# A decoder layer on one core: the residual row before the FFN is formed with the norm's weight multiplied ahead, its transposed float32 copy is taken first, and rows 512 to 1023 go first

## The chip, the core and the metric

The kernel runs on one core of a Trainium2 chip. A core has five engines that work side by side, each through its own instructions in a fixed order: PE (matrix products and transposes), DVE, ACT and POOL (elementwise work) and SP, which issues the DMA transfers here. The products go to PSUM, the other operands lie in SBUF. The metric is the time of one execution in microseconds (us), and lower is better.

## The reference, cut to what matters

```python
def rms_norm(x, g):
    y = xf * lax.rsqrt(jnp.mean(xf * xf, axis=-1, keepdims=True) + NORM_EPS)
    return (y * g.astype(jnp.float32)).astype(x.dtype)
...
mix = hybrid_mixer(rms_norm(h, g_mix_pre[i]), ...)          # ends in concat([attn, c]) @ w_o
h = h + rms_norm(mix, g_mix_post[i])
ffn = conv_gated_ffn(rms_norm(h, g_ffn_pre[i]), ...)
h = h + rms_norm(ffn, g_ffn_post[i])
...
def conv_gated_ffn(xn, w_gate, w_up, dw_w, dw_b, w_down):
    g = causal_depthwise_conv(xn @ w_gate, dw_w, dw_b)       # 3 taps along the sequence
    return (jax.nn.gelu(g, approximate=True) * (xn @ w_up)) @ w_down
```

There are 1024 positions of width 1024, in float32, and D_FF is 2816. The part at stake here is the end of the mixer (the product with `w_o` and the post norm), the residual, the pre norm of the FFN, and the first products of the FFN.

## The kernel before, in words

Each float32 operand of a product is split into a rounded high part and a low part, so that one product becomes three. The 1024 positions are eight rows of tiles of 128 positions; here they are called row 0 to row 7 in the order in which they are worked on, and in the kernel before that is also their place in the sequence. Rows 0 to 3 form one half of 512 positions (`xh[1]`, `xl[1]` serve as `hh[0]`, `hl[0]`), rows 4 to 7 the other (`hh1`, `hl1`).

The program is written for a scheduler, which fixes each engine's order at build time. So the order of the listing is not the order on an engine; the orders quoted below are those of the built programs.

For each row, `wo_mm` makes 24 products on PE into one of two PSUM buffers `ps_w`. Their rounded inputs `ch` (ACT) and `cl` (POOL, four subtractions of 128x128) have two buffers. `wo_post` and `back_h` then do this, and the letters are used from here on:

- **A** (L915, DVE): the partial row from DRAM is added to `ps_w`, which frees the PSUM buffer.
- **J** (L179 on `junk`, ACT): the mean square. **P** (L169, L170, POOL): its reciprocal root, two small instructions.
- **X**: the row of the residual. Before, this is L917 on DVE (`part` times root times weight), and then L918 on POOL (`xr` plus `part`).
- **S** (L179 on `part`, ACT) and **Q** (L169, L170, POOL): the same for the second norm. **F** (L922, DVE): the row times root times weight, into `tmp`.
- **T** (L929, PE): eight transposes into one of two PSUM buffers `ps_h`.
- **H** (L118, ACT): the rounded part `hh`. **L** (L123, DVE): the low part `hl`. **C** (L931, ACT): the float32 copy of the transposed row into `acc`, which is stored to `hT_d`.

The last two rows' T are held back (`late`) behind the first products of the FFN. Those are four sets of 48 products: gate and up of FFN tile 0 (`g0`, `u0`), gate and up of tile 11 (`g1`, `u1`), each set over both halves of the positions, 24 products each. After them the FFN goes over to seven products in place of eight (the first is `ps_ga`). These need sums of blocks of the transposed rows, which `block_sums(j)` on DVE makes from `hT_d[j]` and `hT_d[4 + j]`, read back from DRAM; `sal` is the last kind of block that they write. On DVE the same queue holds the three-tap convolution of the gate (`conv3`, L1092 behind ACT's L1090).

Of the kernel before, what the change touches and what calls it, by code (L numbers as in the profile page):

```python
# [15 lines left out]
F32 = mybir.dt.float32  # L16
# [3 lines left out]
ALU = mybir.AluOpType  # L20
# [72 lines left out]
def layer_kernel(tc, x, xT, pT, pos, vecs, rows, w_inc, w_q, w_kv, w_qb, w_kvb, w_o, w_gu, w_down, w_ple, w_pg, out):  # L93
    nc = tc.nc
    pools = {}

    def popen(name, side="left", space=None):
        kw = dict(name=name, bufs=1, reuse_waits="tile")
        if space is not None:
            kw["space"] = space  # L100
        kw["side"] = side
        cm = tc.tile_pool(**kw)
        pools[name] = (cm, cm.__enter__())
        return pools[name][1]
# [11 lines left out]
    def split(src, hi, lo, scale=None, leng=None):  # L116
        if scale is None:
            nc.scalar.copy(hi, src)  # L118
        else:
            nc.scalar.activation(out=hi, in_=src, func=AF.Copy, scale=scale)  # L120
        if scale is None:
            e = nc.gpsimd if leng == "pool" else nc.vector
            e.tensor_tensor(out=lo, in0=src, in1=hi.bitcast(F32), op=ALU.subtract)  # L123
        else:
            nc.vector.scalar_tensor_tensor(out=lo, in0=src, scalar=scale, in1=hi.bitcast(F32), op0=ALU.mult, op1=ALU.subtract)  # L125

    def mm(ps, l, r, st, sp):
        nc.tensor.matmul(ps, lhsT=l, rhs=r, start=st, stop=sp)  # L128
# [37 lines left out]
    def rstd_of(ms, tag, mul=None):  # L166

        t = small.tile([P, 1], F32, name="rs", tag="rs" + tag, bufs=3)
        nc.gpsimd.tensor_scalar(out=t, in0=ms, scalar1=1.0, scalar2=EPS, op0=ALU.mult, op1=ALU.add)  # L169
        nc.gpsimd.tensor_tensor(out=t, in0=t, in1=mhalf[:, 0:1], op=ALU.pow)  # L170
        if mul is not None:
            nc.gpsimd.tensor_scalar(out=t, in0=t, scalar1=mul, scalar2=0.0, op0=ALU.mult, op1=ALU.add)
        return t

    def msq(src, junk, n, tag, out=None):

        if out is None:
# [17 lines left out]
    acc = [accp.tile([P, S], F32, name=f"acc{m}") for m in range(NCH)]  # L195
# [95 lines left out]
    with tc.high_priority():  # L291
        ps = psv("ps_x")
        for t in range(NT):
            tk = slice(t * P, (t + 1) * P)
# [57 lines left out]
    for i in range(2, 2 * NCH):  # L352
        w = nw
# [30 lines left out]
    def trt(n, **kw):  # L384
        return trg.tile([P, NT, NFQ], F32, name=n, **kw)
# [21 lines left out]
    for a, i, levels in ((al, 3, 0), (ah, 3, 0), (al, 2, 0), (ah, 2, 1), (al, 1, 1), (ah, 1, 1), (al, 0, 1), (ah, 0, 2)):  # L407
        q = trt("pr", tag="pr", bufs=2)
# [20 lines left out]
    def ps1(name):  # L429
        return psA.tile([P, HALF], F32, name=name, tag="s1", bufs=2)  # L430
# [91 lines left out]
    for nm, wh, wl, width, rank, dh, dl in (("k", wkh, wkl, KVW, KVL, kah, kal), ("q", wqh, wql, QL, QL, qah, qal)):  # L522
        stages = []
        for t in range(NT):
            g, tk = t // 4, slice(t % 4 * P, (t % 4 + 1) * P)
# [85 lines left out]
    with tc.high_priority():  # L611
        V2(out=y1, in0=x1, in1=cosT, op=ALU.mult)
        for g in range(2):
            sl = slice(g * HALF, (g + 1) * HALF)
            tmp = ps1("ps_t")
# [275 lines left out]
    def psd(name, i):  # L891
        return psB.tile([P, D], F32, name=name, tag=f"d{i % 2}", bufs=2)
# [3 lines left out]
    hh = [xh[1], hnp.tile([P, KD, HALF], F32R, name="hh1")]  # L896
    hl = [xl[1], hnp.tile([P, KD, HALF], F32R, name="hl1")]
    hp = popen("hp")
    gmix = hp.tile([P, D], F32, name="gmix")
    nc.sync.dma_start(gmix, rows[0:1, :].partition_broadcast(P))  # L900
    gffn = hp.tile([P, D], F32, name="gffn")
    nc.sync.dma_start(gffn, rows[1:2, :].partition_broadcast(P))

    def wo_mm(t):
        ps = psd("ps_w", 0)
        part = hp.tile([P, D], F32, name="part2", tag="part2", bufs=3)
        nc.sync.dma_start(part, mix_d[t])
        xr = hp.tile([P, D], F32, name="xr", tag="xr", bufs=3)
        nc.sync.dma_start(xr, x[t * P:(t + 1) * P, :])
        halves = [slice(0, HALF), slice(HALF, D)]  # L910
        wo_products(ps, list(zip(halves, halves)), 0, *rows_of(0, t, hp, 2))
        return ps, part, xr

    def wo_post(t, ps, part, xr):
        nc.vector.tensor_tensor(out=part, in0=ps, in1=part, op=ALU.add)  # L915
        r = rstd_of(msq(part, pools["wop"][1].tile([P, D], F32, name="junk", tag="rawo", bufs=2), D, "w"), "w")
        nc.vector.scalar_tensor_tensor(out=part, in0=part, scalar=r, in1=gmix, op0=ALU.mult, op1=ALU.mult)  # L917
        nc.gpsimd.tensor_tensor(out=xr, in0=xr, in1=part, op=ALU.add)  # L918
        nc.sync.dma_start(h_d[t], xr)
        r = rstd_of(msq(xr, part, D, "w"), "w")  # L920
        tmp = hp.tile([P, D], F32, name="tmp", tag="tmp", bufs=2)
        nc.vector.scalar_tensor_tensor(out=tmp, in0=xr, scalar=r, in1=gffn, op0=ALU.mult, op1=ALU.mult)  # L922
        return tmp

    def back_h(t, tmp):
        g, tk = t // 4, slice(t % 4 * P, (t % 4 + 1) * P)
        pst = psd("ps_h", 1)
        for k in range(KD):
            nc.tensor.transpose(out=pst[:, k * P:(k + 1) * P], in_=tmp[:, k * P:(k + 1) * P], identity=ident)  # L929
        split(pst.rearrange("p (j q) -> p j q", q=P), hh[g][:, :, tk], hl[g][:, :, tk])  # L930
        nc.scalar.copy(acc[2 + t % 2], pst)  # L931
        nc.sync.dma_start(hT_d[t], acc[2 + t % 2])

    hT_d = dram.tile([NT, P, D], F32, name="hT_d")
    late = []
    nxt = wo_mm(0)
    for t in range(NT):
        cur = nxt
        if t + 1 < NT:
            nxt = wo_mm(t + 1)  # L940
        turned = wo_post(t, *cur)
        if t < NT - 2:
            back_h(t, turned)
        else:
            late.append((t, turned))
# [256 lines left out]
    junk = dp.tile([P, D], mybir.dt.bfloat16, name="junk")  # L1202
# [115 lines left out]
    def h2_trans(t):  # L1318
        pst = psE.tile([P, D], F32, name="ps_ht", tag="ht", bufs=1)
        for k in range(KD):  # L1320
            nc.tensor.transpose(out=pst[:, k * P:(k + 1) * P], in_=h2[t][:, k * P:(k + 1) * P], identity=ident)  # L1321
        th_, tl_ = (t_.rearrange("p (k c) -> p k c", c=P) for t_ in h2b[t % 2])
        split(pst.rearrange("p (j q) -> p j q", q=P), th_, tl_)
        return th_, tl_

    with tc.high_priority():
        nxt = h2_trans(0)
    for t in range(NT):
        th_, tl_ = nxt
        if t + 1 < NT:  # L1330
            nxt = h2_trans(t + 1)
# [3 lines left out]
        r = rstd_of(msq(et, sg, D, "e"), "e", mul=0.5)  # L1335
# [68 lines left out]
```

## Time and profile before

| | |
|---|---|
| times of three runs | 1291.3, 1291.8 and 1297.38 us, median 1291.8 us |
| the profiled execution's own time | 1292.91 us, span from first to last instruction 1291.1 us |
| PE busy | 1230.6 us, 95% of the span |
| DVE, ACT, POOL busy | 71%, 48%, 43% |
| mean granted PE clock | 0.972 of full speed |

The profile is of one execution. An engine that is busy for 95% of the span sets the time nearly everywhere; where it stands still or gets a lower clock, something is to be won. A stage can be bounded by another engine than the whole is, so stages are read by themselves.

### The profile page before, as it was taken

What the parts mean: (1) busy time and instruction counts of PE and PEld (TensorE: products, weight loads), DVE (VectorE), ACT (ScalarE), POOL (GpSimd) and SP (SyncE); (2) the same over time, 40 slices, a digit from 0 to 9 for tenths busy, and PEclk for the clock granted to TensorE, in tenths of its full rate; (3) what the DMA queues carried; (4) which work ended last, traced back from release to release, by engine and by line L of the source; (5) the groups of instructions that cost most, each with busy time, mean ns of one, the idle gap of its engine ahead of it and who ended that gap; (6) DMA issues with size and microseconds to landing.
All of it is one profiled execution on the core that took longest, in us unless ns stands there. A gap on an engine that the chain in (4) does not pass through costs nothing. (4 is left out here: it accounts for less than half of the span.)

```text
span 1291.1 us, 16697 instructions
## 1 busy us (share of the span) xinstructions
PE 1230.6 (95%) x5905; PEld 1032.9 (80%) x5905; DVE 919.2 (71%) x1192; ACT 625.0 (48%) x1117; POOL 553.1 (43%) x588
## 2 busy tenths in 40 slices
PE   9999999889999989699999999999999999997998
PEld 7789987778888878577788888888888888885887
DVE  8399999865566545678887787787777876687343
ACT  6346775576656645454333433333334444463122
POOL 4776954542633348526546555565511200013000
PEclk9999999799999989889999999999999999998999
DMA  6210146534643256554322323331369544452232
GB/s 232 66 54 1 45 164 218 160 110 140 158 105 90 82 191 209 204 168 151 122 97 84 106 87 117 122 121 59 123 215 339 159 142 135 138 169 74 66 98 66
DMA packets 58483, 167.41 MB, mean 130 GB/s; under 512 B 6880, under 2 KB 10336, under 8 KB 56864
## 3 DMA queue, kind: packets, MB, share of 16 engines
q1 hardware_dynamic: 58256, 166.23, 39.4%
q8 instruction: 46, 0.75, 0.3%
q14 instruction: 37, 0.30, 0.1%
q10 hardware_dynamic: 144, 0.12, 0.0%
HBM read 114.42 MB, written 51.90 MB: 129 GB/s over the span
## 5 line engine op out<-in xcount | busy, mean ns | idle before, releaser
L343 DVE SCALAR_TENSOR_TENSOR ps_cv<-c,hvec,ps_cv 128x1023 f32<-128x1023 f32 (+25 forms) x96 | 122.2, 1273 | 2.6
L169 POOL TENSOR_SCALAR rs<-ss 128x1 f32<-128x1 f32 x32 | 16.2, 508 | 242.9 <-ACT junk L179 136.4
L717 POOL TENSOR_SCALAR pr<-pr,sm 128x896 f32<-128x896 f32 (+3 forms) x64 | 47.8, 751 | 123.1 <-DVE sm L716 100.6
L118 ACT CAST xh<-acc 128x512 fp32r<-128x512 f32 x77 | 47.9, 622 | 96.3 <-PE ps_da L1241 42.3
L123 POOL TENSOR_TENSOR kt<-acc,qt 128x512 fp32r<-128x512 f32 x39 | 62.9, 1620 | 43.0 <-ACT qt L118 31.3
L128 PE MATMUL ps_s<-kt,qt 96*128 96x512 f32 (+3 forms) x288 | 71.2, 377 | 9.2 <-ACT pr L715 6.1
L123 POOL TENSOR_TENSOR hl<-acc,hh 128x512 fp32r<-128x512 f32 x40 | 61.5, 1544 | 38.0 <-ACT hh L118 26.3
L1092 DVE SCALAR_TENSOR_TENSOR gt<-gx,vec,gt 128x1023 f32<-128x1023 f32 (+1 forms) x40 | 64.7, 1634 | 13.5 <-ACT gt L1090 13.5
L123 DVE TENSOR_TENSOR xl<-acc,xh 128x512 fp32r<-128x512 f32 x77 | 52.7, 687 | 29.8 <-ACT xh L118 28.6
L1241 PE MATMUL ps_da<-xl,xh 128*128 128x512 f32 x176 | 68.6, 390 | 0.4 <-DVE xl L123 0.4
L1241 PE MATMUL ps_da<-xh,xl 128*128 128x512 f32 x176 | 68.5, 389 | 0.0
L123 DVE TENSOR_TENSOR ptl<-ps_pt,pth 128x512 fp32r<-128x512 f32 (+2 forms) x96 | 50.9, 551 | 23.7 <-ACT pth L118 22.9
L1241 PE MATMUL ps_da<-xh 128*128 128x512 f32 x176 | 66.7, 389 | 0.0
L128 PEld LDWEIGHTS ps_s<-kt,qt 96*128 96x128 f32 x288 | 50.9, 201 | 18.1 <-ACT pr L715 8.4
L715 ACT ACTIVATE pr<-ps_s,mx,qf 128x896 f32<-128x896 f32 (+3 forms) x64 | 53.5, 839 | 22.8 <-DVE mx L712 21.5
L710 DVE TENSOR_REDUCE mx<-ps_s 128x1 f32<-128x896 f32 (+3 forms) x64 | 46.9, 752 | 24.0 <-PE ps_s L128 23.7
L118 ACT CAST pth<-ps_pt 128x512 fp32r<-128x512 f32 (+2 forms) x96 | 43.8, 485 | 25.0 <-PE ps_pt L727 24.6
L128 PE MATMUL ps_pg<-wg 128*128 128x512 f32 x192 | 47.6, 408 | 4.9 <-ACT wg L118 4.9
L128 PE MATMUL ps_c<-xl,wch 128*128 128x512 f32 x128 | 51.6, 404 | 0.3 <-DVE xl L125 0.3
L128 PE MATMUL ps_c<-xh,wcl 128*128 128x512 f32 x128 | 51.4, 401 | 0.0
L1241 PE MATMUL ps_db<-xh,xl 128*128 128x512 f32 x132 | 51.4, 389 | 0.0
L123 POOL TENSOR_TENSOR wx<-acc,wx 128x512 fp32r<-128x512 f32 x21 | 33.4, 1594 | 41.9 <-ACT wx L118 34.8
(623 smaller groups left out, 4007.2 us busy)
## 6 DMA issues: line engine op xcount, KB each, us to landing
acc<-in_w_gu_dram SPq DMA_DIRECT2D x44, 512.0 KB, 4.7
acc<-act_d SPq DMA_DIRECT2D x77, 256.0 KB, 2.8
act_d<-gx SPq DMA_DIRECT2D x22, 512.0 KB, 3.1
bw<-in_w_down_dram SPq DMA_DIRECT2D x32, 256.0 KB, 5.9
act_d<-gt SPq DMA_DIRECT2D x11, 512.0 KB, 2.6
kn_d<-wq SPq DMA_DIRECT2D x8, 512.0 KB, 3.2
qn_d<-wq SPq DMA_DIRECT2D x8, 512.0 KB, 3.7
kt<-kn_d SPq DMA_DIRECT2D x8, 512.0 KB, 5.3
```

The lines of the kernel that those rows point to most:

```text
L118: nc.scalar.copy(hi, src)
L123: e.tensor_tensor(out=lo, in0=src, in1=hi.bitcast(F32), op=ALU.subtract)
L128: nc.tensor.matmul(ps, lhsT=l, rhs=r, start=st, stop=sp)
L169: nc.gpsimd.tensor_scalar(out=t, in0=ms, scalar1=1.0, scalar2=EPS, op0=ALU.mult, op1=ALU.add)
L343: nc.vector.scalar_tensor_tensor(out=pc[:, s_:], in0=c[m][:, :S - s_], scalar=tap(m, s_), in1=pc[:, s_:], op0=ALU.mult, op1=ALU.add)
L710: nc.vector.tensor_reduce(out=mx, in_=ps, axis=AX.X, op=ALU.max, negate=True)
L715: nc.scalar.activation(out=pr[:, :n], in_=ps, func=AF.Exp, scale=qfi, bias=mx, accum_out=sm)
L717: nc.gpsimd.tensor_scalar(out=pr[:, :n], in0=pr[:, :n], scalar1=sm, scalar2=0.0, op0=ALU.mult, op1=ALU.add)
L1092: nc.vector.scalar_tensor_tensor(out=out[:, s_:], in0=src[:, :S - s_], scalar=V("dw", 3 * f + 2 - s_), in1=out[:, s_:], op0=ALU.mult, op1= ...
L1241: nc.tensor.matmul(bank[j], lhsT=l[:, js], rhs=r, start=first and kk == n == 0, stop=kk == HF - 1 and n == 2, skip_group_check=not first)
```

## The change

`wo_post` multiplies the row by the norm's weight in an instruction of its own (called **G** below, L922 after), which needs no root and so can run while ACT makes the mean square. The residual X is then one instruction on DVE (L923), `tmp` times root plus `xr`, and POOL's addition is gone. Of the transposed row the float32 copy C comes first; H and L read this copy in SBUF in place of the PSUM tile. The rows are worked on in the order 4, 5, 6, 7, 0, 1, 2, 3, and the halves of the first FFN products change places with them. Every fourth row has a `part` buffer of its own, and the scratch for J is one fixed buffer.

```diff
+    ROWS = (4, 5, 6, 7, 0, 1, 2, 3)
+    junk_w, part_x = (pools["wop"][1].tile([P, D], F32, name=n, tag="rawo", bufs=2) for n in ("junk", "partx"))
...
-        part = hp.tile([P, D], F32, name="part2", tag="part2", bufs=3)
+        part = part_x if t % 4 == 3 else hp.tile([P, D], F32, name="part2", tag="part2", bufs=3)
...
-        r = rstd_of(msq(part, pools["wop"][1].tile([P, D], F32, name="junk", tag="rawo", bufs=2), D, "w"), "w")
-        nc.vector.scalar_tensor_tensor(out=part, in0=part, scalar=r, in1=gmix, op0=ALU.mult, op1=ALU.mult)
-        nc.gpsimd.tensor_tensor(out=xr, in0=xr, in1=part, op=ALU.add)
+        tmp = hp.tile([P, D], F32, name="tmp", tag="tmp", bufs=2)
+        r = rstd_of(msq(part, junk_w, D, "w"), "w")
+        nc.vector.tensor_tensor(out=tmp, in0=part, in1=gmix, op=ALU.mult)
+        nc.vector.scalar_tensor_tensor(out=xr, in0=tmp, scalar=r, in1=xr, op0=ALU.mult, op1=ALU.add)
...
-        split(pst.rearrange("p (j q) -> p j q", q=P), hh[g][:, :, tk], hl[g][:, :, tk])
-        nc.scalar.copy(acc[2 + t % 2], pst)
-        nc.sync.dma_start(hT_d[t], acc[2 + t % 2])
+        row = acc[2 + t % 2]
+        nc.scalar.copy(row, pst)
+        nc.sync.dma_start(hT_d[t], row)
+        split(row.rearrange("p (j q) -> p j q", q=P), hh[g][:, :, tk], hl[g][:, :, tk])
...
-    ffn_mm(*g0, 0)
-    ffn_mm(*u0, 0)
+    ffn_mm(*g0, 1)
+    ffn_mm(*u0, 1)
...
-    ffn_mm(*g1, 0)
+    ffn_mm(*g1, 1)
     u1 = psd("ps_u", 1), wu_
     for pw in (g0, u0, g1):
-        ffn_mm(*pw, 1)
-    for g in range(2):
+        ffn_mm(*pw, 0)
+    for g in (1, 0):
         ffn_mm(*u1, g)
```

DVE, late rows of the stage. Before, in the built order, the queue holds F (L922), X's first half (L917) and L (L123 from `ps_h`):

```order
L922 SCALAR_TENSOR_TENSOR tmp<-xr,rs,gffn 128x1024
L917 SCALAR_TENSOR_TENSOR part_5235<-part_5235,rs,gmix 128x1024
L123 TENSOR_TENSOR hl_4841<-ps_h,hh_4840 128x8x128
L922 SCALAR_TENSOR_TENSOR tmp<-xr,rs,gffn 128x1024
L917 SCALAR_TENSOR_TENSOR part_5304<-part_5304,rs,gmix 128x1024
```

The same queue after the change, for rows 4 and 5, holds X (L923), L, A (L919), F (L926) and G (L922) in this order:

```order
L923 SCALAR_TENSOR_TENSOR xr<-tmp,rs,xr 128x1024
L123 TENSOR_TENSOR hl_4841<-acc_103,hh_4840 128x8x128
L919 TENSOR_TENSOR part_5163<-ps_w,part_5163 128x1024
L926 SCALAR_TENSOR_TENSOR tmp<-xr,rs,gffn 128x1024
L922 TENSOR_TENSOR tmp<-part_5163,gmix 128x1024
L923 SCALAR_TENSOR_TENSOR xr<-tmp,rs,xr 128x1024
```

So a row has five instructions of full size on DVE in place of four, of which only A still reads PSUM, and L of an older row and A of the next one stand between a row's X and its F.

ACT, the same rows. Before, H (L118 from `ps_h`) comes first and C (L931) after S or J of the next rows:

```order
L118 CAST xh_125<-ps_h 128x8x128
L179 ACTIVATE part_5097,ss<-xr 128x1024
L179 ACTIVATE junk,ss<-part_5166 128x1024
L931 COPY acc_104<-ps_h 128x1024
L179 ACTIVATE part_5166,ss<-xr 128x1024
```

After, S and J are followed by C (L935) and, at once, by H, which reads the copy `acc`:

```order
L179 ACTIVATE part_5095,ss<-xr 128x1024
L179 ACTIVATE junk,ss<-part_5163 128x1024
L935 COPY acc_104<-ps_h 128x1024
L118 CAST hh_4840<-acc_104 128x8x128
L179 ACTIVATE part_5163,ss<-xr 128x1024
```

C no longer stands behind L of its own row, and with it `ps_h` is free.

PE, where the last products of `g1` (weights in `qt`, `kt`; rows in `xh_125`, `xl_127` or `hh_4840`, `hl_4841`) give way to `u1`. Before, all 48 products of `u1` stand here, first those with `xh_125`:

```order
L128 MATMUL ps_g<-hh_4840,kt 128x512
L128 MATMUL ps_u<-xh_125,qt 128x512
L128 MATMUL ps_u<-xl_127,qt 128x512
L128 MATMUL ps_u<-xh_125,kt 128x512
L128 MATMUL ps_u<-xh_125,qt 128x512
```

After the change the first 23 products of `u1` stand elsewhere, behind the first half of `g1` and the last T (L933):

```order
L128 MATMUL ps_g<-hh_4840,qt 128x512
L128 MATMUL ps_g<-hl_4841,qt 128x512
L128 MATMUL ps_g<-hh_4840,kt 128x512
L933 MATMUL ps_h<-ident,tmp 128x128 x8
L128 MATMUL ps_u<-hh_4840,qt 128x512
L128 MATMUL ps_u<-hl_4841,qt 128x512
```

Behind them come 97 products up to `ps_ga`, those of the second half; the last of `g1` is the 74th of them, and 23 products of `u1` follow it in place of 48.

## Rows read from the trace of the kernel before

**Rows 1.** Windows of the stage: busy us (instructions) per engine, granted clock, DMA.

```profile
466.00:516.00 50.00, 48.89 (x224) 40.47 (x224) 22.02 (x19) 23.63 (x58) 36.30 (x54) 0.96 0.53 182
516.00:554.00 38.00, 26.02 (x110) 20.47 (x109) 23.44 (x21) 17.93 (x25) 16.94 (x18) 0.83 0.58 212
```

**Rows 2.** Timeline of PE: start, duration, instruction, [idle before it, releaser].

```profile
520.83 0.76 PE L128 MATMUL ps_g<-xh,wfh 128*128 128x512 f32 x1 [4.67 <-DVE part L915]
...
549.20 1.97 PE L929 MATMUL ps_h<-ident,tmp 128*128 128x128 f32 x8 [4.79 <-ACT acc L931]
552.27 0.79 PE L128 MATMUL ps_g<-hh,wfh 128*128 128x512 f32 x1 [1.10 <-ACT hh L118]
...
558.36 0.40 PE L128 MATMUL ps_g<-hh,wfh 128*128 128x512 f32 x1
...
571.28 0.39 PE L128 MATMUL ps_g<-hh,kt 128*128 128x512 f32 x1
...
582.39 0.39 PE L1086 MATMUL ps_ga<-xh,wx 128*128 128x512 f32 x1
...
589.70 0.50 PE L1086 MATMUL ps_gb<-sal,qt 128*128 128x512 f32 x1 [1.03 <-DVE sal L123]
...
622.59 0.50 PE L1086 MATMUL ps_ud<-sah,qt 128*128 128x512 f32 x1 [2.19 <-DVE v L1018]
```

**Rows 3.** Timeline of POOL, ACT and DVE: one round of the late rows.

```profile
533.26 2.40 POOL L918 TENSOR_TENSOR xr<-xr,part 128x1024 f32<-128x1024 f32 x1 [1.40 <-DVE part L917]
...
535.70 1.06 ACT L179 ACTIVATE part<-xr 128x1024 f32<-128x1024 f32 x1 [0.33 <-POOL xr L918]
...
537.79 1.28 DVE L922 SCALAR_TENSOR_TENSOR tmp<-xr,rs,gffn 128x1024 f32<-128x1024 f32 x1 [3.47 <-POOL rs L170]
...
537.98 1.15 POOL L169 TENSOR_SCALAR rs<-ss 128x1 f32<-128x1 f32 x1 [0.22 <-ACT junk L179]
...
539.79 1.29 DVE L917 SCALAR_TENSOR_TENSOR part<-part,rs,gmix 128x1024 f32<-128x1024 f32 x1 [0.71 <-POOL rs L170]
...
541.15 2.40 POOL L918 TENSOR_TENSOR xr<-xr,part 128x1024 f32<-128x1024 f32 x1 [1.40 <-DVE part L917]
```

**Rows 4.** Timeline of DVE and POOL: rows 0 to 3.

```profile
474.61 1.23 DVE L915 TENSOR_TENSOR part<-ps_w,part 128x1024 f32<-128x1024 f32 x1 [7.74 <-PE ps_w L128]
474.72 1.73 POOL L123 TENSOR_TENSOR cl<-att,ch 128x128 fp32r<-128x128 f32 x4 [4.81 <-ACT ch L118]
...
477.11 0.19 POOL L169 TENSOR_SCALAR rs<-ss 128x1 f32<-128x1 f32 x1 [0.67 <-ACT junk L179]
...
477.96 1.28 DVE L917 SCALAR_TENSOR_TENSOR part<-part,rs,gmix 128x1024 f32<-128x1024 f32 x1 [2.12 <-POOL rs L170]
...
505.68 1.47 DVE L917 SCALAR_TENSOR_TENSOR part<-part,rs,gmix 128x1024 f32<-128x1024 f32 x1 [0.71 <-POOL rs L170]
```

**Rows 5.** Timeline of POOL and DVE where both have SBUF operands at once.

```profile
516.12 2.35 POOL L918 TENSOR_TENSOR xr<-xr,part 128x1024 f32<-128x1024 f32 x1 [1.40 <-DVE part L917]
...
517.10 2.46 DVE L123 TENSOR_TENSOR kt<-acc,qt 128x1024 fp32r<-128x1024 f32 x1
...
520.61 1.21 DVE L123 TENSOR_TENSOR kt<-acc,qt 128x1024 fp32r<-128x1024 f32 x1
...
590.78 4.23 POOL L123 TENSOR_TENSOR kt<-acc,qt 128x512 fp32r<-128x512 f32 x1 [6.43 <-ACT qt L118]
...
593.19 0.68 DVE L1018 TENSOR_TENSOR gx<-gt,gx 128x512 f32<-128x512 f32 x1
```

**Rows 6.** Timeline of ACT and DVE: last copies, block sums and convolution; row 7's A.

```profile
527.82 1.23 DVE L915 TENSOR_TENSOR part<-ps_w,part 128x1024 f32<-128x1024 f32 x1 [2.48 <-DMA part<-mix_d]
...
553.51 1.01 ACT L931 COPY acc<-ps_h 128x1024 f32<-128x1024 f32 x1 [1.29 <-DVE hl L123]
...
572.01 1.20 ACT L1090 ACTIVATE gt<-ps_g,vec 128x1024 f32<-128x1024 f32 x1
...
574.85 1.27 DVE L1092 SCALAR_TENSOR_TENSOR gt<-ps_g,vec,gt 128x1023 f32<-128x1023 f32 x1
```

More of the change, by code (lines that the diff above doesn't have):

```diff
@@ L915, in wo_post @@
         nc.vector.tensor_tensor(out=part, in0=ps, in1=part, op=ALU.add)
-        r = rstd_of(msq(part, pools["wop"][1].tile([P, D], F32, name="junk", tag="rawo", bufs=2), D, "w"), "w")
-        nc.vector.scalar_tensor_tensor(out=part, in0=part, scalar=r, in1=gmix, op0=ALU.mult, op1=ALU.mult)
-        nc.gpsimd.tensor_tensor(out=xr, in0=xr, in1=part, op=ALU.add)
+        tmp = hp.tile([P, D], F32, name="tmp", tag="tmp", bufs=2)
+        r = rstd_of(msq(part, junk_w, D, "w"), "w")
+        nc.vector.tensor_tensor(out=tmp, in0=part, in1=gmix, op=ALU.mult)
+        nc.vector.scalar_tensor_tensor(out=xr, in0=tmp, scalar=r, in1=xr, op0=ALU.mult, op1=ALU.add)
         nc.sync.dma_start(h_d[t], xr)
         r = rstd_of(msq(xr, part, D, "w"), "w")
-        tmp = hp.tile([P, D], F32, name="tmp", tag="tmp", bufs=2)
         nc.vector.scalar_tensor_tensor(out=tmp, in0=xr, scalar=r, in1=gffn, op0=ALU.mult, op1=ALU.mult)
@@ L929, in back_h @@
             nc.tensor.transpose(out=pst[:, k * P:(k + 1) * P], in_=tmp[:, k * P:(k + 1) * P], identity=ident)
-        split(pst.rearrange("p (j q) -> p j q", q=P), hh[g][:, :, tk], hl[g][:, :, tk])
-        nc.scalar.copy(acc[2 + t % 2], pst)
-        nc.sync.dma_start(hT_d[t], acc[2 + t % 2])
+        row = acc[2 + t % 2]
+        nc.scalar.copy(row, pst)
+        nc.sync.dma_start(hT_d[t], row)
+        split(row.rearrange("p (j q) -> p j q", q=P), hh[g][:, :, tk], hl[g][:, :, tk])
     hT_d = dram.tile([NT, P, D], F32, name="hT_d")
     late = []
-    nxt = wo_mm(0)
-    for t in range(NT):
+    nxt = wo_mm(ROWS[0])
+    for n, t in enumerate(ROWS):
         cur = nxt
-        if t + 1 < NT:
-            nxt = wo_mm(t + 1)
+        if n + 1 < NT:
+            nxt = wo_mm(ROWS[n + 1])
         turned = wo_post(t, *cur)
-        if t < NT - 2:
+        if n < NT - 2:
             back_h(t, turned)
```

## The prediction, made before the changed kernel was run

> **What bounds the kernel now.** The page's first view has PE busy for 95% of the span, so only a stage in which PE stands or runs slowly can give time back. The windows show such a stage just where the change is made: PE is busy for 48.89 of 50 us while the products with `w_o` run, but for 26.02 of 38 us from 516 to 554, at a mean granted clock of 0.83 [rows 1]. PE's timeline says what it stood for [rows 2]: 4.67 us for A of row 6, whose `ps_w` buffer `g0` needs; 4.79 us for C of row 6, without which the last T has no `ps_h` buffer; then 1.10 and 1.03 us. Behind the second of these PE was at the lower level (1.2 GHz): the 14 products from 552.27 to 558.36 took 6.09 us, while the 57 from 558.36 to 571.28 took 12.92 us, 0.227 each, at 2.4 GHz. That is 2.9 us lost beside the idle time.
>
> Both waits are on the chain of the rows' norms, which runs over DVE, ACT and POOL. A late round of it goes from POOL's addition at 533.26 to the next at 541.15, 7.89 us [rows 3]: addition 2.40, S 1.24, then J on ACT, whose root P gives X its start 0.72 us after F has ended (537.79 + 1.28 to 539.79). For rows 0 to 3, with `cl` on POOL as well, L917 recurs from 477.96 to 505.68 in three rounds of 9.24 us [rows 4]. PE needs only 24 x 0.227 = 5.4 us for a row's products and some 0.8 for a T (an estimate: half of the 1.97 at the lower level in rows 2, less its overlapped end), 6.2 together. So the chain is the slower one, and PE runs out of buffers.
>
> **The change, part by part.** *X without POOL, G aside.* POOL's 2.40 us leave the chain. X is one instruction on DVE, of L917's kind, 1.28. G costs 1.21, as the subtraction at 520.61 with the same shape and two SBUF inputs [rows 5]. It can run beside J, but the built order puts it behind F.
>
> *What the two engines do to each other.* An operation with two SBUF inputs on DVE and an operation on POOL do not run at once: `kt` on DVE takes 2.46 us while POOL's addition of 516.12 is under way, and 1.21 us alone; POOL's 590.78 subtraction takes 4.23 us, until DVE's unbroken row of additions ends at 593.87 [rows 5]; P's first instruction takes 1.15 us beside F [rows 3], and 0.19 alone [rows 4]. A, with PSUM, does not do this: `cl` took 1.73 us for four beside it [rows 4]. After the change G and L (now from the copy in SBUF) belong to the kind that excludes POOL, so a row has four such instructions, 1.28 + 1.21 + 1.28 + 1.21 = 5.0 us, where it had two.
>
> The Trainium skill, "SBUF — State Buffer", section "Who interferes with whom", states it as an exclusive lock on a port pair for the whole instruction, for VectorE operations with two SBUF inputs against GpSimd operations that read SBUF, and not for one with a PSUM input. The trace agrees with the numbers just given. By this rule alone the change would gain nothing while `cl` runs: the pair's work per row would stay at about 8.2 us (before 2 x 1.28 + 1.73 + 1.46 + 2.40, after 5.0 + 1.73 + 1.46). That result is the second rival below; without the rule it is the first.
>
> *The round after.* Take X's start as zero. DVE goes on with L and A, without a wait, until 3.55; S (1.24) ends at 2.55, Q (0.85, as from 477.11 to 477.96 [rows 4]) fits beside A and ends at 3.45; F ends at 4.8, G at 5.95. J follows A and ends at 4.85, but P must wait for G and gives X its start 0.72 later: a round of 6.65 us against 7.89. With `cl`, which comes ahead of Q on POOL and finds room only from A's start at 2.4, Q ends 1.5 us later and the round is 8.1 against 9.24. So X starts at 478.5 for row 0 (0.5 behind L917's 477.96, as G and `cl` exclude each other), at about 485.9 and 492.9 (no L yet), 501, 509.1 and 517.1 (with `cl`), 526.2 (two subtractions `kt` of 1.21 and their casts lie between) and 533.6. The last F ends at 538.4.
>
> *PE.* The products of row n + 2 need A of row n. A of rows 4, 5 and 6 ends at 504.7, 512.8 and 520.9, so PE stands three times for 1.6 to 1.9 us. Then: 24 products and a T to 527.2, `u0` to 532.6, the next T behind F to 533.8, `g1` to 539.2, the last T to 540.0. Its C (1.01 [rows 6]) frees the buffer of `u1` at 541.1; 23 products end at 546.4, and the 97 of the second half at 568.4. `ps_ga` began at 582.39 [rows 2]: 14.0 us are won up to there.
>
> *C first.* The 4.79 us wait goes, as T no longer waits for H, L and C in a row. What is late next is F, by 0.3 us, and then `u1` by 1.1.
>
> *The halves and `u1`.* Here the gain is cut. The block sums hang on the last C, at 541.1 against 554.52 [rows 6], 13.4 us earlier. But DVE's third convolution instruction (574.85) needs all of `g1`, and only 23 products of `u1` follow `g1` now, in place of 48. `g1` is complete at 546.4 + 74 x 0.227 = 563.2, ACT's 1.20 us [rows 6] follow, and the instruction starts at 564.5: only 10.35 us earlier. The activation behind it takes 0.45 more, and DVE has no gap from there to `sal`. So `ps_gb` gets `sal` at 579.8 against 589.70 [rows 2], 9.9 us earlier, while PE is there at 568.4 + 25 x 0.227 = 574.1. PE's new wait is 5.7 us. It will bring a stretch at the lower level, which costs 2 to 3 us if the one in rows 2 is a measure; but the next wait was 2.19 us at 622.59 [rows 2], for DVE's chain, and this takes it up. Two products of `ps_gd` that stood ahead of the wait stand behind it (0.45), and I leave 0.25 for the rest. Net 9.2.
>
> *At no cost:* the `part` buffer. A of row 7 waited 2.48 us for its load [rows 6]; now the load is issued behind S of row 3, some 15 us ahead of need. The same 512 KB transfers run as before, C's store is issued earlier, and what covers this is that A of row 7 is not what PE waits for; were it late, each us would move the last three T.
>
> *Sum:* 1292.91 - 9.2 = 1283.7 us. The profiled execution is 1.1 us (0.1%) above the median of 1291.8, too little to correct for.
>
> *Bounds.* The prices that no row shows are what DVE and POOL lose to each other and what POOL gets between two DVE instructions. Below: nothing lost, then rows go at PE's 6.2 us. Above: rounds as long as before, 9.24 and 7.89. I take 8.1 and 6.65, as the shares that exclude each other are measured, and the row of 590.78 shows POOL held over several DVE instructions. Ends: 1277.9 and 1289.2, worked out next.
>
> **Rivals.** *PE sets the pace.* If the exclusion costs nothing that PE notices, `g0` starts at 515.6, the second half at 540.6 and `g1` is complete 5.8 us earlier than above: 1283.7 - 5.8 = 1277.9. If the convolution isn't late either, the whole 19.8 us at `ps_ga` stay: 1273.1. For it speaks that POOL loses 2.40 us a row; against it that DVE alone has five instructions, some 6 us, a row.
>
> *The pair of engines sets the pace, no change to be measured.* Rounds stay at 9.24 and 7.89. Then X of row 7 comes at 539.1, 5.5 us later than in the sum, and the time is 1289.2; with the late convolution weighing more, up to 1298. For it speaks the equal sum of 8.2 us; against it that the round of before was longer than that sum, so that the chain, which is cut, counted too.
>
> *The clock, slower than before.* PE stands three times between 503 and 521. If the level falls there and stays low, each us of it costs half a us of products. The gain of 9.2 is gone after 18.4 us at 1.2 GHz, and after 31.4 us the kernel is slower by 0.5%, 1298.4. For it: the windows had 0.83 over 38 us [rows 1]. Against it: the 1.03 us wait at 589.70 is followed by matmuls at full rate, and the level fell behind waits of 4.7 us, not of 1 to 2.
>
> **Chances and numbers.** The forecast (1280 to 1287) has 0.45, PE's pace 0.22, no change 0.23, the clock 0.10. About 0.5%, 6.5 us, is what a measurement of this kernel can tell from no change; four fifths of the forecast's range lie below 1291.8 - 6.5 = 1285.3. So faster 0.36 + 0.22 = 0.58, same 0.09 + 0.23 = 0.32, slower 0.10. The range of 1275 to 1292 leaves out the fast end of the first rival, the slow end of the second and the clock, some 0.2.
>
> **What would show it.** Right: X rounds near 8 and then 6.7 us; no wait of T for C above 1 us; PE idle for 1 to 2 us ahead of the products of rows 6 and 7 and of `ps_g`; `ps_ga` near 568; a wait of some 6 us for `sal`. Wrong: rounds at 6.2 without idle PE (then faster), rounds at 9 (then the second rival), or a granted clock well under 0.9 from 504 to 546. The forecast falls if DVE finds time for the convolution before `g1` is complete, or if the new wait is followed by half speed that nothing takes up.

## The result, and the profile after

The changed kernel takes 1279.19 us (median of four runs, 1273.34 to 1282.71), the kernel before took 1292.38 us beside it. The ratio is 0.9894, with a 95% interval of 0.9869 to 0.9918: faster by 1.1%. The profiled execution took 1277.86 us, 15.05 us less than the one before (1292.91); its span is 1276.1 us. The forecast was 1283.7.

The first view of the page, busy time by engine, and the windows of the same two stretches as in [rows 1], then three more, and below them the last of these stretches in the kernel before (busy us and instructions of PE, PEld, DVE, ACT and POOL, granted clock, DMA share, GB/s):

```profile
PE 1219.0 (96%) x5905; PEld 1023.6 (80%) x5905; DVE 931.0 (73%) x1200; ACT 626.0 (49%) x1117; POOL 540.8 (42%) x580
```

```profile
466.00:516.00 50.00, 48.26 (x237) 40.01 (x236) 34.80 (x29) 28.40 (x64) 37.63 (x54) 1.00 0.71 242
516.00:554.00 38.00, 36.58 (x172) 29.98 (x171) 27.79 (x31) 20.64 (x30) 9.91 (x11) 1.00 0.55 194
554.00:590.00 36.00, 31.56 (x131) 25.38 (x131) 30.22 (x38) 18.55 (x30) 17.50 (x12) 0.95 0.51 173
576.00:582.00 6.00, 5.85 (x19) 4.66 (x20) 4.52 (x9) 0.85 (x3) 0.00 (x0) 0.72 0.51 184
610.00:640.00 30.00, 29.80 (x131) 24.70 (x132) 24.78 (x28) 12.83 (x20) 18.05 (x14) 1.00 0.31 114
```

```profile
610.00:640.00 30.00, 27.81 (x116) 22.48 (x115) 27.21 (x26) 11.41 (x17) 18.60 (x13) 0.94 0.26 92
```

From 516 to 554 PE now does 172 matmuls in place of 110, at full clock. From 554 to 590 it stands for 4.4 us. PE's timeline names what is left (start, duration, instruction, idle time before it and its releaser); these rows answer to [rows 2]:

```profile
510.85 0.70 PE L128 MATMUL ps_w<-qt,ch 128*128 128x512 f32 x2 [0.75 <-DVE part L919]
...
517.81 0.47 PE L128 MATMUL ps_g<-hh,wfh 128*128 128x512 f32 x1 [0.32 <-DVE part L919]
...
536.09 1.04 PE L933 MATMUL ps_h<-ident,tmp 128*128 128x128 f32 x8
538.23 0.50 PE L128 MATMUL ps_u<-hh,qt 128*128 128x512 f32 x1 [1.10 <-ACT acc L935]
...
543.62 0.39 PE L128 MATMUL ps_g<-xh,wfh 128*128 128x512 f32 x1
...
565.61 0.39 PE L1091 MATMUL ps_ga<-xh,wx 128*128 128x512 f32 x1
...
572.66 0.50 PE L1091 MATMUL ps_gb<-sah,qt 128*128 128x512 f32 x1 [1.45 <-ACT sah L118]
576.15 0.53 PE L1091 MATMUL ps_gb<-sal,qt 128*128 128x512 f32 x1 [2.99 <-DVE sal L123]
...
610.21 0.50 PE L1091 MATMUL ps_ud<-sah,qt 128*128 128x512 f32 x1 [1.35 <-DVE v L1023]
```

The waits of 4.67 and 4.79 us are gone, and no T waits in this stage any more. `ps_ga` starts 16.8 us earlier than before, `ps_gb` gets `sal` 13.55 us earlier, and `ps_ud` starts 12.4 us earlier. Another 1.6 us is clock: before, the granted clock from 610 to 640 was 0.94, as nine products behind the 2.19 us wait ran at the lower level; now it is 1.00. So the first product of the down projection, `ps_da`, starts at 954.6 against 968.6, 14.0 us earlier. The last 1 us of the 15.05 lies behind it and was not followed up.

The rounds, on DVE, which answer to [rows 3, 4]: X of rows 0, 3, 4 and 7, with L and the wait for Q of row 3.

```profile
478.46 1.29 DVE L923 SCALAR_TENSOR_TENSOR xr<-tmp,rs,xr 128x1024 f32<-128x1024 f32 x1 [1.26 <-POOL rs L170]
...
499.06 1.28 DVE L923 SCALAR_TENSOR_TENSOR xr<-tmp,rs,xr 128x1024 f32<-128x1024 f32 x1 [0.43 <-POOL rs L170]
500.26 1.48 DVE L123 TENSOR_TENSOR hl<-acc,hh 128x1024 fp32r<-128x1024 f32 x1
501.66 1.21 DVE L919 TENSOR_TENSOR part<-ps_w,part 128x1024 f32<-128x1024 f32 x1
503.84 1.28 DVE L926 SCALAR_TENSOR_TENSOR tmp<-xr,rs,gffn 128x1024 f32<-128x1024 f32 x1 [0.97 <-POOL rs L170]
505.04 1.22 DVE L922 TENSOR_TENSOR tmp<-part,gmix 128x1024 f32<-128x1024 f32 x1
506.70 1.47 DVE L923 SCALAR_TENSOR_TENSOR xr<-tmp,rs,xr 128x1024 f32<-128x1024 f32 x1 [0.43 <-POOL rs L170]
...
529.29 1.28 DVE L923 SCALAR_TENSOR_TENSOR xr<-tmp,rs,xr 128x1024 f32<-128x1024 f32 x1 [0.71 <-POOL rs L170]
```

Seven rounds take 529.29 - 478.46 = 50.83 us, 7.26 each; before, L917 recurred from 477.96 to 539.79 [rows 3, 4], 8.83 each. And the tail of the chain, on ACT and DVE, which answers to [rows 6]: the last C, the first of the sums that read their row back into `acc`, the first convolution instruction on `g1`, and the `sal` that PE waits for. Below them, on SP's queue, the store of the last C and the load that this sum waits for.

```profile
537.16 1.01 ACT L935 COPY acc<-ps_h 128x1024 f32<-128x1024 f32 x1 [3.36 <-PE ps_h L933]
...
549.07 0.69 DVE L1023 TENSOR_TENSOR acc<-acc 128x512 f32<-128x512 f32 x1 [3.44 <-DMA acc<-hT_d]
...
562.13 1.28 DVE L1097 SCALAR_TENSOR_TENSOR gt<-ps_g,vec,gt 128x1023 f32<-128x1023 f32 x1 [0.63 <-ACT gt L1095]
...
575.41 0.68 DVE L123 TENSOR_TENSOR sal<-gx,sah 128x512 fp32r<-128x512 f32 x1
```

```profile
538.20 0.32 SPq L936 DMA_DIRECT2D hT_d<-acc  x1
545.34 0.32 SPq L1028 DMA_DIRECT2D acc<-hT_d  x1
```

This sum starts 10.9 us behind the end of the last C. It is a wait for a buffer: the load overwrites a copy in `acc`, and SP waits 6.8 us for the store of that copy before it issues the load at 545.34. From the sum to `sal` DVE is idle for 1.7 us only. The same sum in the kernel before:

```profile
562.50 0.69 DVE L1018 TENSOR_TENSOR acc<-acc 128x512 f32<-128x512 f32 x1 [3.92 <-DMA acc<-hT_d]
```

### The profile page after: what moved, and what is told of

It reads as the page before. It is cut to its first block, busy times and chain, and to the rows that moved or that the text cites. A ratio compares the mean times of both kernels' runs of the same rounds, so it can differ in the third digit from the quotient of the medians.

```text
span 1276.1 us, 16707 instructions
## 1 busy us (share of the span) xinstructions
PE 1219.0 (96%) x5905; PEld 1023.6 (80%) x5905; DVE 931.0 (73%) x1200; ACT 626.0 (49%) x1117; POOL 540.8 (42%) x580
## 5 line engine op out<-in xcount | busy, mean ns | idle before, releaser
L169 POOL TENSOR_SCALAR rs<-ss 128x1 f32<-128x1 f32 x32 | 21.1, 660 | 240.9 <-ACT junk L179 137.1
L118 ACT CAST xh<-acc 128x512 fp32r<-128x512 f32 (+1 forms) x81 | 52.2, 644 | 96.6 <-PE ps_da L1246 39.0
L123 POOL TENSOR_TENSOR hl<-acc,hh 128x512 fp32r<-128x512 f32 x40 | 61.9, 1556 | 57.6 <-ACT hh L118 26.3
L123 DVE TENSOR_TENSOR xl<-acc,xh 128x512 fp32r<-128x512 f32 (+1 forms) x81 | 57.7, 714 | 32.8 <-ACT xh L118 31.5
L1097 DVE SCALAR_TENSOR_TENSOR gt<-gx,vec,gt 128x1023 f32<-128x1023 f32 (+1 forms) x40 | 64.8, 1633 | 13.5 <-ACT gt L1095 13.5
L123 POOL TENSOR_TENSOR kt<-acc,qt 128x512 fp32r<-128x512 f32 x39 | 59.6, 1534 | 34.8 <-ACT qt L118 23.1
L123 DVE TENSOR_TENSOR ptl<-ps_pt,pth 128x512 fp32r<-128x512 f32 (+2 forms) x96 | 50.9, 551 | 23.1 <-ACT pth L118 22.4
L118 ACT CAST pth<-ps_pt 128x512 fp32r<-128x512 f32 (+2 forms) x96 | 43.8, 485 | 24.4 <-PE ps_pt L727 24.0
L118 ACT CAST hh<-acc 128x512 fp32r<-128x512 f32 (+1 forms) x44 | 28.9, 661 | 52.7 <-PE ps_ga L1091 16.8
L1246 PE MATMUL ps_db<-xl,xh 128*128 128x512 f32 x132 | 51.3, 389 | 0.0
```

The costliest lines, as they stand in the source:

```text
L1097: nc.vector.scalar_tensor_tensor(out=out[:, s_:], in0=src[:, :S - s_], scalar=V("dw", 3 * f + 2 - s_), in1=out[:, s_:], op0=ALU.mult, op1= ...
L1246: nc.tensor.matmul(bank[j], lhsT=l[:, js], rhs=r, start=first and kk == n == 0, stop=kk == HF - 1 and n == 2, skip_group_check=not first)
```

## The experiments

The medians of the kernel before lie between 1291.4 and 1292.83 us beside the different kernels, and the profiled executions differ before the stage too: their first A begins between 469.3 and 476.5. So the last columns are counted from the first A of the same profile (474.61 before, 474.70 after): the last C, the first convolution instruction on `g1`, the last `sal` on DVE, and the first `ps_da`. This last number holds all that the stage and its aftermath win or lose; the three kernels in which PE has the same order (after, x3, z2) agree in it within 0.4 us.

| kernel | median | ratio to before (95%) | last C | conv | last sal | ps_da |
|---|---|---|---|---|---|---|
| before | 1292.38 | | 78.9 | 100.2 | 116.8 | 494.0 |
| after | 1279.19 | 0.9894 (0.9869 to 0.9918) | 62.5 | 87.4 | 103.1 | 479.9 |
| x1 old residual | 1296.39 | 1.0038 (1.002 to 1.0056) | 76.8 | 103.0 | 118.7 | 495.4 |
| x2 copy last | 1277.44 | 0.9905 (0.9883 to 0.9926) | 64.7 | 87.9 | 103.5 | 479.2 |
| x3 rows in order | 1277.2 | 0.9906 (0.9884 to 0.9929) | 62.3 | 88.0 | 103.4 | 480.3 |
| x4 gate early | 1279.96 | 0.9915 (0.989 to 0.9939) | 62.3 | 86.7 | 106.5 | 481.0 |
| y1 residual alone | 1279.62 | 0.9896 (0.987 to 0.9922) | 64.8 | 87.8 | 104.3 | 480.1 |
| y2 addition on DVE | 1287.17 | 0.9961 (0.9939 to 0.9984) | 71.0 | 95.9 | 111.6 | 487.7 |
| y3 rows kept | 1280.61 | 0.9897 (0.9872 to 0.9922) | 62.4 | 87.4 | 103.7 | 482.0 |
| y4 rows kept, gate early | 1279.42 | 0.9903 (0.9876 to 0.9929) | 62.4 | 86.8 | 105.7 | 482.2 |
| z1 slots moved | 1281.0 | 0.9908 (0.9884 to 0.9933) | 62.4 | 86.8 | 104.6 | 480.3 |
| z2 three part buffers | 1278.15 | 0.9874 (0.9847 to 0.9901) | 62.4 | 87.3 | 103.0 | 480.0 |
| z3 split from PSUM | 1275.38 | 0.9867 (0.9841 to 0.9893) | 60.7 | 83.4 | 101.1 | 476.3 |
| w1 PSUM and rows kept | 1277.64 | 0.9892 (0.9864 to 0.9919) | 60.9 | 83.2 | 99.7 | 477.8 |

My theory: the shorter rounds are the gain, and part of it is given back at `sal`. The rivals: the gain is the early copy or the order of the rows; or the turns of DVE and POOL set the pace.

### Which part of the change is the gain

**x1.** The changed kernel with the old `wo_post`:

```diff
-        nc.vector.tensor_tensor(out=tmp, in0=part, in1=gmix, op=ALU.mult)
-        nc.vector.scalar_tensor_tensor(out=xr, in0=tmp, scalar=r, in1=xr, op0=ALU.mult, op1=ALU.add)
+        nc.vector.scalar_tensor_tensor(out=part, in0=part, scalar=r, in1=gmix, op0=ALU.mult, op1=ALU.mult)
+        nc.gpsimd.tensor_tensor(out=xr, in0=xr, in1=part, op=ALU.add)
```

> The changed kernel with the old residual step (weight times row times root on DVE, then POOL's addition), all else as changed. Theory, the shorter round of the rows is what wins: X recurs again in 9.2 us while cl runs and in about 7.9 us late, the last row's F ends some 6 to 7 us later than the 534.0 us after the change, the second half starts near 550, and the time is 1284 to 1287. Rival, the gain comes from the early float32 copy and the order of the rows: within 2 us of the changed kernel's 1279.

It is 0.4% slower than before: more than the theory had, and the rival is out. The addition on POOL takes longer than its 2.40 us [rows 3], since L now reads SBUF too: the late additions follow each other in 8.8 us, not the 7.9 of the theory. And PE waits 7.38 us for H, which ACT does only behind S and J. POOL's and PE's timelines of x1:

```profile
513.83 3.25 POOL L922 TENSOR_TENSOR xr<-xr,part 128x1024 f32<-128x1024 f32 x1 [1.40 <-DVE part L921]
...
520.29 0.80 PE L128 MATMUL ps_g<-hh,wfh 128*128 128x512 f32 x1 [7.38 <-ACT hh L118]
```

**x2.** The changed kernel with the old end of a row, H and L first:

```diff
-        nc.scalar.copy(row, pst)
-        nc.sync.dma_start(hT_d[t], row)
-        split(row.rearrange("p (j q) -> p j q", q=P), hh[g][:, :, tk], hl[g][:, :, tk])
+        split(pst.rearrange("p (j q) -> p j q", q=P), hh[g][:, :, tk], hl[g][:, :, tk])
+        nc.scalar.copy(acc[2 + t % 2], pst)
+        nc.sync.dma_start(hT_d[t], acc[2 + t % 2])
```

> The changed kernel with the old end of a row (H and L from PSUM, the float32 copy C behind them). Theory: X's rounds stay near 7.0 to 7.5 us, the last T waits again for C (up to 4.8 us), but the built order has all 48 products of u1 behind g1, and these cover part of the wait for sal; 1279 to 1283. Rival, the early copy is half of the gain or more: 1285 to 1289. Rival, the copy in SBUF makes DVE and POOL exclude each other and costs: 1274 to 1278.

No change that shows (`ps_da` at 479.2 against 479.9). The median is 1.6 us under the theory's range and lies in that of the last rival, that the copy in SBUF costs; this run can't settle that, and z3 takes it up. The last T waits for C again, but for 1.58 us, not 4.79. The built order has the 48 products of `u1` behind `g1`, and the wait for `sal` is 2.04 us. PE's timeline of x2:

```profile
534.65 1.09 PE L933 MATMUL ps_h<-ident,tmp 128*128 128x128 f32 x8 [1.58 <-ACT acc L935]
...
575.14 0.79 PE L1090 MATMUL ps_gb<-sal,qt 128*128 128x512 f32 x1 [2.04 <-DVE sal L123]
```

**x3.** `for n, t in enumerate(range(NT))` and the halves of before.

> The changed kernel with the rows in the order 0 to 7 and the halves of the first FFN products as before. The built order of PE is the same but for the names of the halves. Theory, the order of the rows plays no part: 1278 to 1280.5. Rival, it does (a buffer of the rounded rows comes free earlier): 1283 or more.

The order of the rows is worth nothing that shows (480.3 against 479.9); the median lies 0.8 us below the range given.

**y1.** The kernel before with the new `wo_post` (L919 to L926 after) alone.

> The kernel before with nothing but the new residual step (G aside, X on DVE without POOL's addition). Theory, this step is the whole gain, as the changed kernel without it is slower than before, and without the early copy or the order of the rows as fast as with them: 1276 to 1281, rounds of X near 7 us, cl x4 on POOL in 2.7 us. Rival, the early copy gives part of it once the rounds are short: 1283 or more.

The residual step alone gives the whole gain, 480.1 against 479.9. Together with x1 this settles which part it is.

**y2.** The two old steps, but both on DVE:

```diff
-        nc.vector.tensor_tensor(out=tmp, in0=part, in1=gmix, op=ALU.mult)
-        nc.vector.scalar_tensor_tensor(out=xr, in0=tmp, scalar=r, in1=xr, op0=ALU.mult, op1=ALU.add)
+        nc.vector.scalar_tensor_tensor(out=part, in0=part, scalar=r, in1=gmix, op0=ALU.mult, op1=ALU.mult)
+        nc.vector.tensor_tensor(out=xr, in0=xr, in1=part, op=ALU.add)
```

> The changed kernel with the residual formed in the old two steps (row times root times weight, then the addition), but both on DVE: POOL's addition is gone, G is not drawn ahead. DVE has as many full-size instructions as after the change. Theory, taking POOL's 2.4 us off the chain is what counts and G beside the mean square saves at most its 1.2 us a row: rounds 0 to 1.2 us longer than after, 1279 to 1287. Rival, G aside is what counts: rounds of 8.5 or more and 1288 or more.

At 1287.17 it lies between the theory's range and the rival's. The residual on DVE recurs in (531.61 - 475.00) / 7 = 8.09 us, 0.83 more than after. Of the 14.1 us at `ps_da`, the addition's move to DVE gives 494.0 - 487.7 = 6.3, and the weight drawn ahead the other 7.8: about half and half, with the same number of DVE instructions. (Against x1, from which y2 differs by this move, it gives 7.7. The medians put it lower: y2 is 5.5 us below the kernel before beside it, of 13.2 for the whole change.) PE waits 3.30 us for F once, as its timeline of y2 shows, and behind that 1.80 us for A and 1.47 for L:

```profile
513.34 1.94 PE L933 MATMUL ps_h<-ident,tmp 128*128 128x128 f32 x8 [3.30 <-DVE tmp L926]
```

**z2.** `part = hp.tile(..., bufs=3)` for every row.

> The changed kernel without the fourth part buffer (three in rotation, as before). The built order of PE is the same. Theory, the buffer is worth nothing, since rows are no longer late enough to wait for it: 1277 to 1281. Rival, A of row 7 waits for its load again (2.5 us before) and the last three T with it: 1280 to 1283.

The buffer is worth nothing that shows: 480.0 and 479.9.

### What DVE and POOL lose to each other

**z3.** C first, but H and L read the PSUM tile:

```diff
-        split(row.rearrange("p (j q) -> p j q", q=P), hh[g][:, :, tk], hl[g][:, :, tk])
+        split(pst.rearrange("p (j q) -> p j q", q=P), hh[g][:, :, tk], hl[g][:, :, tk])
```

> The changed kernel with the float32 copy C first, but H and L reading the PSUM tile again. Theory, L in SBUF and POOL's cl take turns and that costs 1 us a round while cl runs: four cl take 2.7 us in place of 3.7, rounds of X fall to about 7.0, the last X comes 0.5 to 1.5 us earlier counted from the first A, but sal, not the rounds, decides what is left: 1276 to 1280. Rival, the turns set the pace of the whole stage: 1272 to 1275.

First POOL's timeline after the change, four `cl` and then the second of them by itself; below them the same place in z3:

```profile
499.17 3.74 POOL L123 TENSOR_TENSOR cl<-att,ch 128x128 fp32r<-128x128 f32 x4
...
500.62 1.44 POOL L123 TENSOR_TENSOR cl<-att,ch 128x128 fp32r<-128x128 f32 x1
```

```profile
500.25 1.28 DVE L923 SCALAR_TENSOR_TENSOR xr<-tmp,rs,xr 128x1024 f32<-128x1024 f32 x1 [0.71 <-POOL rs L170]
500.53 2.58 POOL L123 TENSOR_TENSOR cl<-att,ch 128x128 fp32r<-128x128 f32 x4 [0.31 <-ACT ch L118]
501.46 1.22 DVE L123 TENSOR_TENSOR hl<-ps_h,hh 128x1024 fp32r<-128x1024 f32 x1
...
506.91 1.28 DVE L923 SCALAR_TENSOR_TENSOR xr<-tmp,rs,xr 128x1024 f32<-128x1024 f32 x1 [0.43 <-POOL rs L170]
```

With L in SBUF, X, one `cl`, L and one `cl` take turns: the `cl` beside L takes 1.44 us, L 1.48 in place of 1.22, and four `cl` 3.74. In z3 four take 2.58, and X recurs in 6.66 us in place of 7.64. In x2 and y1, where L reads PSUM too, four `cl` beside X and L take 2.7 as well. The last X is 2.0 us earlier (52.6 against 54.6 from the first A), a bit more than expected, the last C 1.8, and `ps_da` 3.6. The time lies between the theory's range and the rival's. What is shown is that the turns cost 0.6 to 1.0 us in each of the three rounds with `cl` and an L (6.79, 6.66 and 6.65 us against 7.41, 7.64 and 7.41), and that this reaches the last C. That all 3.6 us come from the turns is not shown, since two more things differ. PE's order does: all 48 products of `u1` follow `g1` in z3. And the row read back is there at 70.4 us from the first A, 4.0 earlier than after, of which 1.8 are the store's (5.3 us to landing, not 7.1). PE's wait for `sal` is gone.

### What holds sal

**x4.** `for pw in (g0, g1, u0)` in place of `(g0, u0, g1)`.

> The changed kernel with the second halves in the order g0, g1, u0, so that g1 is complete 24 products (5.4 us) earlier. Theory of the prediction, the late convolution holds sal: the wait for sah and sal (4.4 us together) falls to 1.5 or less, the time is 1275 to 1277. Rival, DVE has no gap from the block sums read back at 549.1 to sal at 575.4 but 1.7 us, so the read-back row and DVE's work behind it set sal and g1 does not: within 1 us of the changed kernel, and sal at most 1 us earlier.

No gain, and the last `sal` is 3.4 us later, but the convolution did not come early either: its first instruction on `g1` is at 86.7 (87.4 after). So the run tests neither side. The two rows of ACT in x4 say what it waited for: a weight cast that waits for `g1`'s buffer `qt` stands ahead of `sah`, and the second activation starts when `u0` is complete, not `g1` (555.9).

```profile
555.84 0.62 ACT L118 CAST qt<-wt 128x512 fp32r<-128x512 f32 x1 [4.03 <-PE ps_g L128]
...
561.06 1.21 ACT L1095 ACTIVATE gt<-ps_g,vec 128x1024 f32<-128x1024 f32 x1 [1.40 <-PE ps_u L128]
```

**y3.** The sums take rows 6 and 7 from SBUF (rows 2 and 3 of the sequence):

```diff
-        nc.sync.dma_start(hT_d[t], row)
+        if t not in (2, 3):
+            nc.sync.dma_start(hT_d[t], row)
...
-        r0, r1 = (ftile("gx", 2, S) if j % 2 == 0 else acc[2 + i] for i in range(2))
-        nc.sync.dma_start(r0, hT_d[j])
+        r0, r1 = (ftile("gx", 2, S) if j != 1 and not (i == 0 and j > 1) else acc[2 + (i if j < 2 else j % 2)] for i in range(2))
+        if j < 2:
+            nc.sync.dma_start(r0, hT_d[j])
...
-    for j in range(4):
+    for j in (2, 3, 0, 1):
```

> The changed kernel, but the block sums of the last two rows take these rows from the copies that lie in SBUF, in place of storing them and reading them back, and are the first sums. The read-back ends 10.9 us behind the last copy C in the changed kernel. Theory, two chains come together behind it, the read-back and the convolution that waits for g1: the sums start some 6 to 10 us earlier, but the third convolution instruction still waits for g1 (562), DVE stands there for several us, and sal is at most 1.5 us earlier: 1277 to 1279. Rival, the read-back alone holds sal: sal 5 us or more earlier, 1273 to 1275.

The sums are earlier, and DVE then stands 5.29 us for the activation of `g1`, as the theory had it; `sal` gains nothing. The time (1280.61) is above the theory's range: PE waits 3.80 us for `sah` and 1.17 for `sal`, and `ps_da` is 2.1 us later than after. DVE's timeline of y3:

```profile
544.53 2.48 DVE L123 TENSOR_TENSOR sal<-acc,sah 128x512 fp32r<-128x512 f32 x4
...
557.90 1.28 DVE L1099 SCALAR_TENSOR_TENSOR gt<-ps_g,vec,gt 128x1023 f32<-128x1023 f32 x1 [5.29 <-ACT gt L1097]
```

**y4.** y3 with the order of x4.

> The kernel with the rows kept in SBUF for the block sums, and g1 completed 24 products earlier as well. Theory, with both chains drawn ahead sal comes 4 us or more earlier than in the changed kernel, the waits of ps_gb and ps_gc fall from 4.4 to under 1.5 together, and the time is 1272 to 1276. Rival, DVE's own work (26 us from the sums to sal) is the limit whatever starts it: no more than 1 us below the changed kernel.

The time fits the rival, but not for the rival's reason, and the theory is not tested either: `sal` is 2.6 us later than after. ACT waits 10.44 us for `g1`'s buffer with `sah` behind it, and DVE 7.45 us for `sah`. ACT and DVE of y4:

```profile
553.29 0.62 ACT L118 CAST qt<-wt 128x512 fp32r<-128x512 f32 x1 [10.44 <-PE ps_g L128]
...
554.46 3.18 DVE L123 TENSOR_TENSOR sal<-acc,sah 128x512 fp32r<-128x512 f32 x4 [7.45 <-ACT sah L118]
```

**z1.** y4 with the slots of the seven products' weights in another order, `extra`, the four of `a21h`, `a21l`, then `wo01` with `i` in `(1, 0)`.

> Rows kept in SBUF, g1 early, and the seven products' weights take the free slots in another order, so that on ACT no weight that waits for g1's own buffer stands ahead of sah, as it did for 10.4 us in the run before this one. Theory, three things arrive together (read-back, convolution, ACT's queue) and with all three drawn ahead sal comes 3 us or more earlier, counted from the first A: 1272 to 1276. Rival, DVE's own work between the sums and sal is the limit: sal less than 2 us earlier, 1277 to 1280.

ACT's queue is free now, but the second activation again waits for `u0`, 8.99 us, and DVE 6.93 for it. The time (1281.0) is above both ranges. The theory did not get its early convolution, so its forecast failed; that DVE's own work is the limit is not shown by it either. ACT and DVE of z1:

```profile
559.55 1.21 ACT L1096 ACTIVATE gt<-ps_g,vec 128x1024 f32<-128x1024 f32 x1 [8.99 <-PE ps_u L128]
...
560.79 1.28 DVE L1098 SCALAR_TENSOR_TENSOR gt<-ps_g,vec,gt 128x1023 f32<-128x1023 f32 x1 [6.93 <-ACT gt L1096]
```

Why that activation waits for `u0` stays open. So what an early convolution on `g1` is worth was never measured.

**w1.** z3 with the rows kept as in y3.

> The two edits that point the same way together: H and L read the PSUM tile again (rounds of 6.7 us), and the block sums of the last two rows take the copies that lie in SBUF. Counted from the first A, the run with H and L from PSUM alone began the down products at 476.3 us, the changed kernel at 479.9. Theory, with the read-back gone the third convolution instruction waits for g1 alone, which is complete some 3 us ahead of where that instruction began in that run: down products at 473 to 475.5, the time 1271 to 1276. Rival, what is left is the chain behind sal (2.3 us before ps_ud), which does not depend on it: 476 to 478, and 1275 to 1279.

The rival: `ps_da` at 477.8, 1277.64 us. The last `sal` is 1.4 us earlier than in z3 and wins nothing; PE waits 2.33 us for `v` before `ps_ud`, as in z3 (2.25). So z3 has the earliest `ps_da` of all; its lead of 3.6 us over the changed kernel is seen from the first A of one profile each, while the intervals of their ratios overlap, so that its time is lower is not shown.

## Why the prediction was right, and where its sizes were off

The time lies inside the range, and the mechanism holds: shorter rounds, PE's two long waits gone, something given back at `sal`. The sum was too small: it said 9.2 us and the profile 15.05. Of the difference 3.65 us are `sal` (13.55 us earlier, not 9.9), 1.6 the clock behind the former 2.19 us wait, and 1 lies behind `ps_da`, less 0.45 that went on the way from `sal` to `ps_ud`. The median, 1279.19, is just below the forecast's own 1280 to 1287; it lies in the wider range because that takes in most of the first rival, so part of being right is luck. Term by term:

- **The rounds** were mis-sized. By the sum's X times they were 7.4, 7.0, 8.1, 8.1, 8.0, 9.1 and 7.4; they took 6.67, 6.52, 7.41, 7.64, 7.41, 8.07 and 7.11, and the last X began at 529.29, not 533.6. Of these 4.3 us, 1.7 lie in the three rounds with `cl` and L. The step that failed there is that POOL "finds room only from A's start": `cl` takes turns with X and L, so Q is done 0.2 to 0.4 us earlier, and P's first instruction slips in between F and G (X starts 0.44 us behind G's end, not 0.72). Another 1.2 lie in the first two rounds and 1.0 in the one with the two `kt`, which were priced too high as well. Where the exclusion was switched off for L (z3) the rounds with `cl` and L fell by 0.6 to 1.0 us, so it exists, at a lower price than I gave it. The row of 590.78 [rows 5], on which I had rested the choice, is one POOL instruction beside DVE's unbroken row of 512-wide additions, not the pattern here.
- **The lock.** The Trainium skill, "SBUF — State Buffer", section "Who interferes with whom", was weighed in the prediction. The trace agrees with it on which operations exclude each other: a `cl` beside L from SBUF takes 1.44 us and L 1.48, while L from PSUM takes its 1.22 (z3). By the sum of 8.2 us that I had made from it the gain would have been nothing; rounds of 7.4 to 7.6 us are shorter than that sum, so the second rival is out. The sum counted all four `cl` as exclusive, while two of them ran beside A, which reads PSUM.
- **PE's three stalls** of 1.6 to 1.9 us were 0.75 and 0.32 us and one none, as A of rows 5 and 6 ended at 510.71 and 517.66, not 512.8 and 520.9. The second half began at 543.62, not 546.4.
- **C first** has its 1.1 us wait at `u1` to the hundredth (1.10). But that the 4.79 us wait goes is for the most part no merit of C: without the early copy it is 1.58 (x2), since the rows come sooner, and the time shows no difference.
- **The halves and u1.** I had the convolution on `g1` at 564.5 as what holds `sal`; it came at 562.13, as `g1` was done 2.8 us sooner, and waited only 0.63 there. The row read back arrives just as late: its first sum begins at 549.07, 13.43 us earlier than before (562.50), and DVE needs 27.02 us from there to the end of the `sal` that PE waits for (27.15 before). So `sal`, 13.55 us earlier, moved with this chain. y3 shows the other one: with the read-back gone the convolution waits 5.29 us and `sal` is no earlier. So the step named one of two chains that end together. My 13.4 us for the sums came out by luck: the last C ends 16.35 us earlier than before, and the store and load behind it take 10.9 us, not 8.0. The wait was 1.45 + 2.99 = 4.4 us against 5.7.
- **The clock.** The stretch at the lower level came (0.72 from 576 to 582): nine products took 3.74 us from 576.15 to 579.89, at 0.227 each 2.04, so 1.7 us lost against 2 to 3. `ps_ud` won 12.4 us, and 1.6 us more came from the stretch behind the former 2.19 us wait, which I had not counted as a loss of before: there the nine products from 622.92 to 626.56 took 3.64 us.
- **The part buffer** costs and gives nothing that shows, as said (z2).

Of the rivals, "PE sets the pace" (1277.9) named nearly the measured time, but not its way: PE still waits for A, and the second half began midway between its 540.6 and the forecast's 546.4. The clock rival is out: 1.00 from 466 to 554. But my reason against it, that the level fell "behind waits of 4.7 us, not of 1 to 2", holds for the kernel before only: in x2 the eight products from 536.85 to 540.35, behind waits of 1.58 and 1.10 us with one T between them, took 3.50 us, 1.82 at 0.227 each.

## What to carry to other kernels

Take an operand that needs no result of a reduction (a norm's weight) out of the instruction that waits for it: at an equal count of instructions it gave half of this gain. Before crediting one of several edits, run the whole without it, and the one that is left alone: two of the three main edits here gave nothing that shows. Where a buffer wait vanishes, look for the chains that end together behind it: drawing one ahead (y3) gained nothing as long as the other stood, and drawing both ahead did not come about here (y4, z1).

## What the runs showed of the hardware

Beside X and L, two DVE instructions with two SBUF operands each, the queue of `cl` on POOL was not held until DVE paused: one `cl` got through behind each, in some 0.3 us (the `cl` from 500.62 ended at 502.06, L at 501.74), and DVE's next instruction was 0.2 us longer (1.47 and 1.48 in place of 1.28 and 1.22). The kernel before shows another pattern: its POOL subtraction of 590.78 took 4.23 us beside a row of 512-wide DVE additions [rows 5]. What decides between the two is not shown. One POOL addition of 1024 elements grew from 2.40 to 3.25 us beside one L (x1).
